# A two-layer mixer block on one core: VectorE's convolution sums in PSUM, the convolution's chunks projected ahead of the pool's, and 15 of 31 taps on GpSimd

## The chip, the cores and the metric

One NeuronCore of a Trainium2 chip runs the whole program in one launch. The metric is the device time of that launch in microseconds (us), the median of several runs. Engines are named as in the profile: PE is TensorE, DVE is VectorE, ACT is ScalarE, POOL is GpSimd, SP starts the transfers.

## What is computed

A sequence of 256 tokens with 2048 features passes two layers. Each is a mixer and a gated feed-forward block with residual sums and RMS norms. The change touches only the mixer of the first layer:

```python
def conv_pool_mixer(x, norm_g, w_in, conv_w, conv_b, ln_g, ln_b, w_pool, pool_scale, w_out):
    h = rms_norm(x, norm_g)
    u = h @ w_in
    a_val = u[..., :D_CONV]
    a_gate = u[..., D_CONV:2 * D_CONV]
    b_in = u[..., 2 * D_CONV:]
    a = a_val * jax.nn.sigmoid(a_gate)
    a = causal_depthwise_conv(a, conv_w) + conv_b
    a = jax.nn.silu(layer_norm(a, ln_g, ln_b))
    p = multiscale_pool(b_in, w_pool, pool_scale)
    return jnp.concatenate([a, p], axis=-1) @ w_out
```

D_CONV is 1024 and the causal convolution has 31 taps. The pool makes windowed means (2, 4, 8, 16 tokens) minus the value, in four groups of 256 features, and each group has a 256x256 product of its own.

## The kernel before

Features lie along the 128 partitions and the 256 tokens along the free dimension, so an activation of 2048 features is 16 chunks of 128x256. Weights come as 128x128 blocks in fp32, in the order of their use. A piece of 8 blocks is split by ACT into a rounded half (`hi`, line 109) and by DVE into the rest (`lo = w - hi`, line 110). In the first mixer a block costs PE three products of 256 columns: hi*hi (line 155), hi*lo (156) and lo*hi (157). So PE can't finish a block before DVE has made the `lo` of its piece. Six buffers each hold `hi` and `lo` pieces: `hi` of piece i can be written when PE is done with piece i-6. Pieces 0 to 2 hold 1, 3 and 4 blocks, all later ones 8, so that piece i is PE's stretch number i-2 of 8 blocks, counted from 0. Below, a "stretch of eight" is such a stretch.

The first mixer has 656 blocks, 82 stretches of eight. Stretches 0 to 7 are the four first chunks (value and gate of convolution chunks 0 and 1). Then `M0_ORDER` (line 34) says in which order the other chunks of the first product come: a convolution chunk is a value and a gate accumulator (two stretches each), a pool group is two accumulators. Stretches 48 and 49 are the pool's own products from `cat` (line 448), 50 to 65 the half of the output projection that reads the pool (`project(xs, ...)`, line 497), 66 to 81 the half that reads the convolution (line 500). The feed-forward block begins behind them with PE's first product of line 152.

The other engines work beside that:

- `gated` (line 403): DVE scales value and gate out of PSUM (line 310), ACT takes the sigmoid, DVE multiplies both into `a_in` (line 407).
- The convolution of a pair of chunks is cut in two. For its first taps ACT multiplies (`prod`, line 364, four buffers) and POOL adds to `conv` in SBUF (line 366). For the others DVE multiplies and adds in one instruction into `side` (line 377; the first tap is line 375). Line 381 adds `side` to `conv`.
- `pooled` (line 418): DVE scales out of PSUM into `xp` (line 425), makes the windowed sums (`sw`, lines 430 to 434), ACT rounds to `cat` (line 436) and DVE makes the rest (line 437). PE's stretches 48 and 49 read `cat`; their results go to `xs` by ACT (line 188) and DVE (line 189).
- The layer norm of the convolution (lines 457 to 485) runs beside stretches 50 to 65 and ends with Silu on ACT (line 482), `cat` (line 484) and its rest on DVE (line 485). Stretch 66 reads it.

`CONV` (line 76) says how many taps of which chunks go to POOL; `PACE` (line 77) how many blocks of products are issued between two steps of the side work. A scheduler orders each engine's instructions from that; each engine then runs its list in order. [...]

Of the kernel before, what the change touches and what calls it, by code (L numbers as in the profile page):

```python
# [11 lines left out]
F32 = mybir.dt.float32  # L12
# [5 lines left out]
P = 128  # L18
T = 256
# [11 lines left out]

# the order of the first product's output after its first four chunks: chunks of the convolution,
# and groups of the pool
M0_ORDER = (
    ("conv", 2), ("conv", 3), ("pool", 3), ("conv", 4), ("conv", 5), ("pool", 2), ("conv", 6),
    ("pool", 1), ("pool", 0), ("conv", 7),
)
POOL_ORDER = [i for kind, i in M0_ORDER if kind == "pool"]
POOL_CHUNKS = [2 * g + j for g in POOL_ORDER for j in range(2)]

# columns of the per-feature vectors, one column per chunk of 128 features
VECS = {}
# [9 lines left out]

# blocks of 128x128 weights in the order of their use
N_BLOCKS = 24 * NC + 16 + NC * NC + 2 * (2 * NF * NC + NC * NF) + 48 * NC + NC * NC
# [10 lines left out]
UNIT_AT = [sum(UNITS[:u]) for u in range(len(UNITS))]  # L65
# units are split into halves in pieces: (unit, first block, blocks)
PIECE = 8
PIECES = [(u, o, min(PIECE, n - o)) for u, n in enumerate(UNITS) for o in range(0, n, PIECE)]
# pieces that are split, and units that are loaded, before they are needed
LOOK = 4  # L70
AHEAD = 1
# products that the tensor engine turns over before the first operands are there
WARM = 9
# taps of each pair of chunks of the long convolution that GpSimd adds up (VectorE takes the rest),
# and the pace of the work beside the matrix products in blocks a step
CONV = {1: (0, 2, 20), 3: (2, 2, 20), 5: (4, 2, 19), 6: (6, 1, 18), 7: (7, 1, 18)}
PACE = {"pool2": 4.6, "dve2": 6.5, "pool1": 2.5, "dve1": 2.2, "ln": 4.0, "wait": 1.0, "now": 0.0}


@with_exitstack  # L80
def block_kernel(ctx: ExitStack, tc: tile.TileContext, xT: bass.AP, vec: bass.AP, wall: bass.AP, out: bass.AP):
# [5 lines left out]
    tmp = ctx.enter_context(tc.tile_pool(name="tmp", bufs=2))  # L87
    ps = ctx.enter_context(tc.tile_pool(name="ps", bufs=7, space=PSUM))
    ps_st = ctx.enter_context(tc.tile_pool(name="ps_st", bufs=1, space=PSUM))

# [1 line left out]
    loaded, ready = {}, {}  # L92
    cursor = [0, 0]  # next block, piece of the next block

# [33 lines left out]

# [1 line left out]
    queues = {name: deque() for name in ("pool", "dve", "ln", "wait")}  # L130
# [28 lines left out]
    def matmul_chunks(xs, ks, n=1, wide=False, behind=None):  # L159
        """n chunks of 128 output features: hi*hi + hi*lo + lo*hi. When wide, columns 0:T hold  # L160
        hi*hi and T:2T the cross terms."""
        accs = [ps.tile([P, 2 * T], F32, name="acc") for _ in range(n)]
        for i, k in enumerate(ks):
            first, last = i == 0, i == len(ks) - 1
            for acc in accs:
                hi, lo = next_block()
                product(acc, hi, lo, xs[:, k, :], first, last, wide)
                tick()
            if behind is not None:
                behind(k)  # L170
        return accs

    phase = [None]  # the pool of the part of the kernel that is being built

# [7 lines left out]
    def split(dst, src, scale=None):  # L182
        """dst[:, :T], dst[:, T:] = fp32r halves of src (times a scale per feature)."""
        if scale is None:
            nc.scalar.copy(dst[:, :T], src)
            nc.vector.tensor_tensor(out=dst[:, T:], in0=src, in1=dst[:, :T], op=ALU.subtract)
        else:
            nc.scalar.activation(dst[:, :T], src, AF.Copy, scale=scale)  # L188
            nc.vector.scalar_tensor_tensor(out=dst[:, T:], in0=src, scalar=scale, in1=dst[:, :T], op0=ALU.mult, op1=ALU.subtract)

# [1 line left out]
    v = const.tile([P, NVEC], F32, name="v")  # L192
# [8 lines left out]
    nc.gpsimd.memset(ones, 1.0)  # L201
    # the tensor engine's clock rises after some microseconds of work
    idle = ps_st.tile([P, P], F32, name="idle", tag="st")
# [13 lines left out]
    def rsqrt_of(*totals, scale, halves=False):  # L217
        """(scale * sum over features and over totals + EPS) ** -0.5 per token, in every partition,
        if asked for in two halves. Tokens lie along the partitions in between."""
        st = ps_st.tile([P, 2], F32, name="st", tag="st")  # L220
# [19 lines left out]
    def over_features(x):  # L240
        """Sum over the partitions, in every partition."""
        st = ps_st.tile([P, T], F32, name="st", tag="st")
        nc.tensor.matmul(st, ones, x, start=True, stop=True)
        return st

    class Norm:
        """RMS norm: h * gain goes into xs chunk by chunk; the factor per token follows."""

# [28 lines left out]
        def square2(self, c):  # L277
            """A pair of chunks."""
            into = tmp.tile([P, 2, T], F32, name="sum2" if c == 0 else "sq2", tag="sum2" if c == 0 else "gate", bufs=1 if c == 0 else 2)
            nc.scalar.activation(into, h[:, c : c + 2, :], AF.Square)  # L280
            if c:
                nc.gpsimd.tensor_tensor(out=self.pairs, in0=self.pairs, in1=into, op=ALU.add)
            else:
                self.pairs = into
                self.sums = [into[:, 0, :], into[:, 1, :]]
# [7 lines left out]
    def project(src, ks, norm=None, wide=False, narrow_end=False):  # L293
        """h += src @ weights, and the next norm behind it."""
        for n in range(NC):
            if narrow_end and n == NC - 1:
                wide = False
            (acc,) = matmul_chunks(src, ks, wide=wide)
            if wide:
                t = phase[0].tile([P, T], F32, name="cross", bufs=3)  # L300
                nc.scalar.copy(t, acc[:, T:])
                nc.vector.tensor_tensor(out=h[:, n, :], in0=h[:, n, :], in1=t, op=ALU.add)
            nc.vector.tensor_tensor(out=h[:, n, :], in0=acc[:, :T], in1=h[:, n, :], op=ALU.add)
            if norm is not None:
                norm.add(n)
# [9 lines left out]

# [1 line left out]
    norm = Norm("mix_norm_e")  # L317
# [27 lines left out]
    every = range(NC)  # L345
    with tc.tile_pool(name="m0", bufs=1) as m0:
        pad = CW - 1
# [8 lines left out]
        def tap(c, n, k):  # L356
            """GpSimd's taps of n chunks."""
            dst = conv[:, c : c + n, :] if k == 0 else m0.tile([P, 2, T], F32, name="prod", bufs=4)[:, :n, :]
# [9 lines left out]
        def side_tap(c, n, k, first):  # L368
            """VectorE's taps, in a sum of their own."""
            if k == first:  # L370
                sides[c] = m0.tile([P, 2, T], F32, name="side", bufs=2)
            for j in range(n):
                src, wt, dst = a_in[:, c + j, k : k + T], col("conv_w_e", (c + j) * CW + k), sides[c][:, j, :]
                if k == first:
                    nc.vector.tensor_scalar(out=dst, in0=src, scalar1=wt, scalar2=None, op0=ALU.mult)  # L375
                else:
                    nc.vector.scalar_tensor_tensor(out=dst, in0=src, scalar=wt, in1=dst, op0=ALU.mult, op1=ALU.add)  # L377
# [11 lines left out]
        def convolve(c, n, taps):  # L389
            """The causal convolution of n chunks."""  # L390
            left = [2]
# [5 lines left out]

            later("pool", f"pool{n}", *(partial(tap, c, n, k) for k in range(taps)))
            later("dve", f"dve{n}", *(partial(side_tap, c, n, k, taps) for k in range(taps, CW)))
            for name in ("pool", "dve"):  # L400
# [17 lines left out]
        def pooled(g):  # L418
            """Windowed means minus the value, for a group of the pool."""
            w = WINDOWS[g]  # L420
# [29 lines left out]

        # layer norm over the features of the convolution, beside the pool's output projection
        state = {}
# [66 lines left out]

# [1 line left out]
    after = Norm("mix_norm_o")  # L521
    swiglu(norm, after)

# [1 line left out]
    norm = Norm("ffn_norm1")  # L525
# [25 lines left out]

# [1 line left out]
    last = Norm("final_norm", final=True)  # L553
# [17 lines left out]
def _blocks(w):  # L571
    """[K, N] -> [N/128, K/128, 128, 128]: output chunk, input chunk, input, output."""
    k, n = w.shape
# [3 lines left out]
def _cols(a):  # L577
    """[N] -> [128, N/128]"""
    return a.reshape(-1, P).T
# [69 lines left out]
```

## Time and profile before

| | before |
|---|---|
| median of 3 runs | 2149.49 us (2149.3 to 2149.75) |
| profiled execution, first to last instruction | 2148.9 us |
| PE busy in it | 2095.9 us, 98% |
| DVE, ACT, POOL busy | 1456.4, 1068.2, 202.2 us |

The page gives the span of the profiled execution and no time of its own for what lies around the span; the median of the runs is 0.6 us above it. Of the span, the first mixer takes the first 306.5 us; there PE is not always busy, and from there to the end it is.

### The profile page before, as it was taken

To read this page: it belongs to the slowest core of one execution; us is meant where nothing else is said; L and a number is where in the kernel's file an instruction comes from. 1 tells how busy PE (TensorE), PEld (TensorE's weight loads), DVE (VectorE), ACT (ScalarE), POOL (GpSimd) and SP (SyncE) were. 2 spreads that over 40 slices of the span, in tenths; PEclk is the share of its full clock that TensorE was granted. 3 is DMA by queue.
4 is the path that set the end of the run, shared out by engine and by line. 5 is a ranking of instruction groups with operands and counts; after the bars stand their busy time and mean duration, and the time that the engine had idled before them with its cause. 6 is when DMAs were issued, how large, how long until landed. Compare 5 with 4: busy or idle time off the path is not lost.

```text
span 2148.9 us, 31546 instructions
## 1 busy us (share of the span) xinstructions
PE 2095.9 (98%) x12564; PEld 1869.5 (87%) x12564; DVE 1456.4 (68%) x1952; ACT 1068.2 (50%) x1595; POOL 202.2 (9%) x210
## 2 busy tenths in 40 slices
PE   8787999999999999999999999999999999999997
PEld 8787998888888888888888888888888888888887
DVE  7999886666555666666677777766666556666554
ACT  7655665444444444445444444554444444444553
POOL 3766420000000000001000000100000000000011
PEclk9889999999999999999999999999999999999999
DMA  7234455555555555555455555555555555555551
GB/s 280 83 134 157 160 200 190 187 186 196 187 186 195 183 190 196 185 188 194 179 196 184 189 197 184 188 184 189 196 187 187 195 180 193 196 184 189 196 180 75
DMA packets 56851, 393.43 MB, mean 183 GB/s; under 512 B 6400, under 2 KB 7424, under 8 KB 9984
## 3 DMA queue, kind: packets, MB, share of 16 engines
q1 hardware_dynamic: 56704, 391.42, 51.1%
q8 instruction: 98, 1.61, 0.3%
q14 instruction: 49, 0.40, 0.1%
HBM read 389.30 MB, written 2.10 MB: 182 GB/s over the span
## 4 chain that ended last, share of the span: by engine, by line
PE 89%; DVE 8%; issue 1%; ACT 1%; DMA 0%; SPq 0%; DVEq 0%
PE acc L152 56%; PE acc L153 29%; DVE side L377 3%; DVE lo L110 2%; PE acc L157 1%; PE acc L156 1%; PE acc L155 1%; DVE sw L430 0%; ACT xs L188 0%; ACT hi L109 0%; DMA h<-in_xT 0%; DVE a_in L407 0%; DVE h L559 0%; DVE side L375 0%; DVE conv L381 0%
## 5 line engine op out<-in xcount | busy, mean ns | idle before, releaser
L110 DVE TENSOR_TENSOR lo<-w,hi 128x1024 fp32r<-128x1024 f32 (+1 forms) x740 | 921.9, 1247 | 632.5 <-ACT hi L109 628.7
L109 ACT CAST hi<-w 128x1024 fp32r<-128x1024 f32 (+1 forms) x740 | 775.7, 1050 | 949.1 <-PE acc L152 622.4
L152 PE MATMUL acc<-xs,hi 128*128 128x512 f32 x3584 | 1243.3, 391 | 0.0
L153 PE MATMUL acc<-xs,lo 128*128 128x256 f32 x3584 | 1003.9, 280 | 0.0
L152 PEld LDWEIGHTS acc<-xs,hi 128*128 128x128 f32 x3584 | 670.3, 187 | 146.9
L153 PEld LDWEIGHTS acc<-xs,lo 128*128 128x128 f32 x3584 | 677.3, 189 | 0.1
L152 PE MATMUL acc<-y,hi 128*128 128x512 f32 x1386 | 485.2, 393 | 0.0
L153 PE MATMUL acc<-y,lo 128*128 128x256 f32 x1386 | 386.1, 279 | 0.0
L152 PEld LDWEIGHTS acc<-y,hi 128*128 128x128 f32 x1386 | 259.4, 187 | 62.1
L153 PEld LDWEIGHTS acc<-y,lo 128*128 128x128 f32 x1386 | 259.7, 187 | 0.4
L273 POOL TENSOR_TENSOR sumsq<-sumsq,sq 128x256 f32<-128x256 f32 x56 | 57.5, 1026 | 1587.8 <-ACT sq L271 1587.8
L157 PE MATMUL acc<-xs,lo 128*128 128x256 f32 x512 | 150.3, 302 | 31.4 <-DVE lo L110 31.2
L155 PE MATMUL acc<-xs,hi 128*128 128x256 f32 x512 | 151.3, 299 | 3.3 <-ACT hi L109 3.3
L156 PE MATMUL acc<-xs,hi 128*128 128x256 f32 x512 | 150.6, 297 | 0.0
L157 PEld LDWEIGHTS acc<-xs,lo 128*128 128x128 f32 x512 | 103.7, 206 | 34.5 <-DVE lo L110 34.3
L366 POOL TENSOR_TENSOR conv<-conv,prod 128x512 f32<-128x512 f32 (+1 forms) x90 | 124.0, 1379 | 62.8 <-ACT prod L364 56.9
L155 PEld LDWEIGHTS acc<-xs,hi 128*128 128x128 f32 x512 | 105.8, 207 | 3.8 <-ACT hi L109 3.7
L156 PEld LDWEIGHTS acc<-xs,hi 128*128 128x128 f32 x512 | 105.7, 207 | 0.1
L152 PE MATMUL acc<-z,hi 128*128 128x512 f32 x256 | 89.6, 393 | 0.0
L177 ACT COPY cross<-acc 128x256 f32<-128x256 f32 x224 | 81.7, 365 | 0.0
L377 DVE SCALAR_TENSOR_TENSOR side<-a_in,v,side 128x256 f32<-128x256 f32 x86 | 77.3, 919 | 0.4
L153 PE MATMUL acc<-z,lo 128*128 128x256 f32 x256 | 71.3, 279 | 0.0
(116 smaller groups left out, 1172.9 us busy)
## 6 DMA issues: line engine op xcount, KB each, us to landing
w<-in_wall SPq DMA_DIRECT2D x365, 1024.0 KB, 4.8
w<-in_wall SPq DMA_DIRECT2D x7, 512.0 KB, 7.1
h<-in_xT SPq DMA_DIRECT2D x7, 256.0 KB, 7.2
out<-h SPq DMA_DIRECT2D x3, 512.0 KB, 2.7
v<-in_vec SPq DMA_DIRECT2D x1, 260.0 KB, 6.6
h<-in_xT SPq DMA_DIRECT2D x2, 128.0 KB, 2.6
w<-in_wall SPq DMA_DIRECT2D x1, 256.0 KB, 3.9
out<-h SPq DMA_DIRECT2D x2, 128.0 KB, 1.9
```

Of the source, the lines that this page charges most:

```text
L109: nc.scalar.copy(hi[:, : n * P], w)
L110: nc.vector.tensor_tensor(out=lo[:, : n * P], in0=w, in1=hi[:, : n * P], op=ALU.subtract)
L152: nc.tensor.matmul(acc, hi, x, start=first, stop=False, skip_group_check=True)
L153: nc.tensor.matmul(acc[:, T:], lo, x[:, :T], start=False, stop=last, skip_group_check=True)
L155: nc.tensor.matmul(acc[:, :T], hi, x[:, :T], start=first, stop=False)
L156: nc.tensor.matmul(acc[:, :T], hi, x[:, T:], start=False, stop=False)
L157: nc.tensor.matmul(acc[:, :T], lo, x[:, :T], start=False, stop=last)
L177: nc.scalar.copy(t, acc[:, T:])
L273: nc.gpsimd.tensor_tensor(out=self.sums[0], in0=self.sums[0], in1=sq, op=ALU.add)
L366: nc.gpsimd.tensor_tensor(out=conv[:, c : c + n, :], in0=conv[:, c : c + n, :], in1=dst, op=ALU.add)
L377: nc.vector.scalar_tensor_tensor(out=dst, in0=src, scalar=wt, in1=dst, op0=ALU.mult, op1=ALU.add)
```

## The change

`side` moves from SBUF to PSUM: a pool of two banks, open during the first mixer alone. For that the accumulators get five banks instead of seven, in the whole kernel. `M0_ORDER` puts all convolution chunks ahead of all pool groups (the weights lie in memory in that order, so that transfers are the same). `CONV` makes four pairs of chunks of 15 POOL taps and 16 DVE taps each, where it had three pairs (20, 20 and 19 taps on POOL) and two single chunks (18 each). So POOL adds 56 times 512 columns (before: 56 times 512 and 34 times 256), and DVE makes 128 side taps of 256 columns (before: 94). `PACE` follows.

```diff
 M0_ORDER = (
-    ("conv", 2), ("conv", 3), ("pool", 3), ("conv", 4), ("conv", 5), ("pool", 2), ("conv", 6),
-    ("pool", 1), ("pool", 0), ("conv", 7),
+    ("conv", 2), ("conv", 3), ("conv", 4), ("conv", 5), ("conv", 6), ("conv", 7), ("pool", 3),
+    ("pool", 2), ("pool", 1), ("pool", 0),
 )
...
-CONV = {1: (0, 2, 20), 3: (2, 2, 20), 5: (4, 2, 19), 6: (6, 1, 18), 7: (7, 1, 18)}
-PACE = {"pool2": 4.6, "dve2": 6.5, "pool1": 2.5, "dve1": 2.2, "ln": 4.0, "wait": 1.0, "now": 0.0}
+CONV = {1: (0, 2, 15), 3: (2, 2, 15), 5: (4, 2, 15), 7: (6, 2, 15)}
+PACE = {"pool": 6.8, "dve": 6.4, "ln": 3.0, "wait": 1.0, "now": 0.0}
...
-    ps = ctx.enter_context(tc.tile_pool(name="ps", bufs=7, space=PSUM))
+    ps = ctx.enter_context(tc.tile_pool(name="ps", bufs=5, space=PSUM))
...
-    with tc.tile_pool(name="m0", bufs=1) as m0:
+    with tc.tile_pool(name="m0", bufs=1) as m0, tc.tile_pool(name="ps_side", bufs=2, space=PSUM) as ps_side:
...
-                sides[c] = m0.tile([P, 2, T], F32, name="side", bufs=2)
+                sides[c] = ps_side.tile([P, 2, T], F32, name="side")
```

The instruction lists of all engines are the same before the first side taps and from the feed-forward block on. Three places in between matter below. The first is ACT in the convolution: how many `prod` (two make one POOL add) stand between two `hi` casts. Before, at the third pair:

```order
L362 ACTIVATE conv<-a_in,v 128x256
L364 ACTIVATE prod<-a_in,v 128x256 x6
L109 CAST hi<-w 128x1024 x2
L364 ACTIVATE prod<-a_in,v 128x256 x4
L109 CAST hi<-w 128x1024
L364 ACTIVATE prod<-a_in,v 128x256 x4
```

Now, at the second pair:

```order
L362 ACTIVATE conv<-a_in,v 128x256
L364 ACTIVATE prod<-a_in,v 128x256 x2
L109 CAST hi<-w 128x1024
L364 ACTIVATE prod<-a_in,v 128x256 x4
L109 CAST hi<-w 128x1024
L364 ACTIVATE prod<-a_in,v 128x256 x4
```

The rate there is four `prod`, two adds, a piece in both. Now all 112 `prod` stand between the casts of pieces 17 and 47, about two adds a piece for 30 pieces; before, they ran on among the later pieces.

The second place is DVE at the end of the pool, just ahead of PE's stretches 48 and 49. Before, the last chunk there was a convolution chunk (`val`, `gate`), and the last group's `cat` was done ahead of its gate:

```order
L310 TENSOR_TENSOR val<-acc,rstd 128x256
L377 SCALAR_TENSOR_TENSOR side<-a_in,v,side 128x256
L434 SCALAR_TENSOR_TENSOR pm<-sw,xp 128x512
L110 TENSOR_TENSOR lo<-w,hi 128x1024
L381 TENSOR_TENSOR conv<-conv,side 128x256
L437 TENSOR_TENSOR cat<-pm,cat 128x2x256
L387 TENSOR_TENSOR total<-total,conv 128x256
L110 TENSOR_TENSOR lo<-w,hi 128x1024
L310 TENSOR_TENSOR gate<-acc,rstd 128x256
```

Now the last group's sums and the `cat` of the two last groups come behind its last accumulator, with side taps and a `lo` between them:

```order
L430 TENSOR_TENSOR sw<-xp 128x2x256
L377 SCALAR_TENSOR_TENSOR side<-a_in,v,side 128x256 x2
L434 SCALAR_TENSOR_TENSOR pm<-sw,xp 128x512
L189 SCALAR_TENSOR_TENSOR xs<-acc,v,xs 128x256
L432 TENSOR_TENSOR sw<-sw,corr 128x2
L377 SCALAR_TENSOR_TENSOR side<-a_in,v,side 128x256 x2
L110 TENSOR_TENSOR lo<-w,hi 128x1024
L189 SCALAR_TENSOR_TENSOR xs<-acc,v,xs 128x256
L434 SCALAR_TENSOR_TENSOR pm<-sw,xp 128x512
L437 TENSOR_TENSOR cat<-pm,cat 128x2x256
L377 SCALAR_TENSOR_TENSOR side<-a_in,v,side 128x256 x2
L437 TENSOR_TENSOR cat<-pm,cat 128x2x256
```

The third place is ACT at the end of the layer norm, ahead of PE's stretch 66. Before, the last `hi` in front of Silu was that of piece 71, and two more stood among the casts to `cat`:

```order
L109 CAST hi<-w 128x1024 x3
L482 ACT_TABLE_LOAD
L482 ACTIVATE conv<-conv,v 128x256 x6
L484 CAST cat<-conv 128x2x256
L482 ACTIVATE conv<-conv,v 128x256 x2
L109 CAST hi<-w 128x1024
L484 CAST cat<-conv 128x2x256 x2
```

Now it is that of piece 73, and none stands among the casts:

```order
L109 CAST hi<-w 128x1024 x3
L482 ACT_TABLE_LOAD
L482 ACTIVATE conv<-conv,v 128x256 x6
L484 CAST cat<-conv 128x2x256
L482 ACTIVATE conv<-conv,v 128x256 x2
L484 CAST cat<-conv 128x2x256 x3
```

So Silu now stands behind two more pieces, and the last of them takes the buffer of piece 67, which is PE's stretch 65.

## Rows read from the trace of the kernel before

**Rows 1.** The page: busy time, share of the span and instructions of each engine.

```profile
PE 2095.9 (98%) x12564; PEld 1869.5 (87%) x12564; DVE 1456.4 (68%) x1952; ACT 1068.2 (50%) x1595; POOL 202.2 (9%) x210
```

**Rows 2.** Windows: length, busy PE, PEld, DVE, ACT, POOL (instructions), granted clock, DMA.

```profile
47.66:73.58 25.92, 25.92 (x219) 25.92 (x218) 24.38 (x24) 17.09 (x35) 20.80 (x14) 1.00 0.35 111
73.58:211.80 138.22, 102.99 (x723) 99.98 (x722) 138.01 (x152) 81.60 (x153) 85.81 (x62) 0.87 0.35 125
211.80:306.50 94.70, 93.95 (x778) 93.22 (x778) 85.04 (x121) 63.22 (x102) 35.73 (x34) 0.99 0.52 185
306.50:406.50 100.00, 100.00 (x581) 88.22 (x580) 64.80 (x97) 51.34 (x75) 0.17 (x1) 1.00 0.52 184
```

**Rows 3.** Waits, 46 to 212 us: who waited for whom, total, times, longest.

```profile
PE acc L157 <- DVE lo L110: 29.3, 10, 6.2
PE acc L155 <- DVE gate L310: 4.0, 1, 4.0
```

**Rows 4.** DVE by line and shape, 46 to 212 us: busy and mean ns.

```profile
L377 DVE SCALAR_TENSOR_TENSOR side<-a_in,v,side 128x256 f32<-128x256 f32 x74 | 68.8, 955 | 0.2
L110 DVE TENSOR_TENSOR lo<-w,hi 128x1024 fp32r<-128x1024 f32 x40 | 60.8, 1521 | 0.0
L425 DVE TENSOR_TENSOR xp<-acc,rstd 128x256 f32<-128x256 f32 x8 | 3.3, 412 | 0.0
L189 DVE SCALAR_TENSOR_TENSOR xs<-acc,v,xs 128x256 fp32r<-128x256 f32 x3 | 1.3, 469 | 0.0
L387 DVE TENSOR_TENSOR total<-total,conv 128x256 f32<-128x256 f32 x1 | 0.4, 410 | 0.0
```

**Rows 5.** POOL by line and shape, 46 to 212 us.

```profile
L366 POOL TENSOR_TENSOR conv<-conv,prod 128x512 f32<-128x512 f32 x56 | 87.0, 1555 | 45.1 <-ACT prod L364 41.6
L366 POOL TENSOR_TENSOR conv<-conv,prod 128x256 f32<-128x256 f32 x17 | 19.4, 1143 | 5.5 <-ACT prod L364 4.3
```

**Rows 6.** DVE's timeline: start, us to the last end, what, how many merged.

```profile
74.88 1.21 DVE L110 TENSOR_TENSOR lo<-w,hi 128x1024 fp32r<-128x1024 f32 x1
76.02 0.41 DVE L310 TENSOR_TENSOR gate<-acc,rstd 128x256 f32<-128x256 f32 x1
76.35 1.26 DVE L377 SCALAR_TENSOR_TENSOR side<-a_in,v,side 128x256 f32<-128x256 f32 x3
77.53 1.21 DVE L110 TENSOR_TENSOR lo<-w,hi 128x1024 fp32r<-128x1024 f32 x1
...
87.66 5.77 DVE L377 SCALAR_TENSOR_TENSOR side<-a_in,v,side 128x256 f32<-128x256 f32 x4
```

**Rows 7.** PE's timeline at the starts of stretches 11 and 50 and of the feed-forward block.

```profile
47.66 0.28 PE L155 MATMUL acc<-xs,hi 128*128 128x256 f32 x1
...
211.79 0.41 PE L155 MATMUL acc<-xs,hi 128*128 128x256 f32 x1
212.01 0.41 PE L156 MATMUL acc<-xs,hi 128*128 128x256 f32 x1
...
306.48 0.40 PE L152 MATMUL acc<-xs,hi 128*128 128x512 f32 x1
```

**Rows 8.** DVE's timeline: `lo` of piece 17, up to which its list is hardly changed.

```profile
45.99 1.23 DVE L110 TENSOR_TENSOR lo<-w,hi 128x1024 fp32r<-128x1024 f32 x1
```

**Rows 9.** Timelines of DVE and ACT at the end of the layer norm.

```profile
254.69 2.50 DVE L480 TENSOR_TENSOR conv<-conv,lr 128x512 f32<-128x512 f32 x4
261.30 0.69 DVE L485 TENSOR_TENSOR cat<-conv,cat 128x512 fp32r<-128x512 f32 x1 [2.30 <-ACT cat L484]
...
255.33 1.05 ACT L109 CAST hi<-w 128x1024 fp32r<-128x1024 f32 x1 [2.26 <-PE acc L156]
257.69 3.07 ACT L482 ACTIVATE conv<-conv,v 128x256 f32<-128x256 f32 x6
260.66 0.60 ACT L484 CAST cat<-conv 128x512 fp32r<-128x512 f32 x1
265.10 0.62 ACT L484 CAST cat<-conv 128x512 fp32r<-128x512 f32 x1
```

More of the change, by code (lines that the diff above doesn't have):

```diff
@@ L396, in end @@
                     later("ln", "now", partial(convolved, c, n))
-            later("pool", f"pool{n}", *(partial(tap, c, n, k) for k in range(taps)))
-            later("dve", f"dve{n}", *(partial(side_tap, c, n, k, taps) for k in range(taps, CW)))
+            later("pool", "pool", *(partial(tap, c, n, k) for k in range(taps)))
+            later("dve", "dve", *(partial(side_tap, c, n, k, taps) for k in range(taps, CW)))
             for name in ("pool", "dve"):
```

## The prediction

> **What bounds the kernel now.** First the page: PE is busy 98% of the span [rows 1], so only the little that PE does not do can be won. The windows say where that lies. From 47.66 to 73.58 us PE runs nine stretches of eight (216 products) in 25.92 us, 2.88 us each, at the full granted clock [rows 2]. From 73.58 to 211.80 us it runs 30 stretches, which at that pace take 86.4 us, in 138.22 us: 51.8 us are lost. There DVE is busy 138.01 of the 138.22 us and the granted clock is 0.87 on the mean. From 211.80 to 306.50 us the last 32 stretches take 94.70 us, some 3 us over their pace, and behind 306.50 us PE is never idle. So the most that any change of the first mixer's middle can bring is some 52 us.
>
> Next the waits of that stretch: PE stands before its lo products, for DVE's `lo`, 29.3 us in ten waits, and 4.0 us once for an accumulator that DVE had not read [rows 3]. DVE is late. Why, the groups say: a side tap of 256 columns takes 955 ns on the mean [rows 4], but on the timeline three of them begin 0.39 us apart at 76.35 us, and four at 87.66 us 1.42 us apart ((5.77-1.5)/3) [rows 6]. At 87.66 us POOL is adding, at 76.35 us it is not. A POOL add and a DVE instruction with two operands in SBUF take turns, and a turn of POOL costs DVE 1.42-0.39 = 1.03 us for 512 columns. `lo` suffers likewise: 1521 ns on the mean [rows 4] against 1.21 at 74.88 us [rows 6]. `xp`, which reads one operand from PSUM, takes 412 ns beside the same adds [rows 4]. The excess of side taps and `lo` alone is 68.8-74x0.47 = 34 and 60.8-40x1.21 = 12 us, 46 us over 73 adds [rows 5], 0.63 us an add; with the smaller groups of that view (first taps, `a_in`, sums of 512 columns), counted in the same way, 61 us and 0.84.
>
> **The change, step by step.** The prices of DVE are spacings on the undisturbed timeline [rows 6]: `lo` 1.14 us, 256 columns of two tensors 0.33, a side tap 0.39 to 0.40, and 0.60 for 512 columns (four in 2.50 us at 254.69 us [rows 9]).
>
> 1. *Side taps in PSUM.* A tap then has one operand in SBUF, as `xp` has, so I take it out of the turns. The trace has no DVE write to PSUM. The nearest row is line 189, which reads an accumulator, multiplies and subtracts: 469 ns [rows 4], what an undisturbed side tap takes. So I take 0.396 us a tap. The cheap end is 0.33 (a plain sum of 256 columns); the dear end is 0.60, as if the read and the write of 256 columns in one bank followed each other.
>
> A tensor in PSUM costs DVE no more than one in SBUF by the rows: 412 ns for `xp`, 410 for `total` [rows 4]. [...]
>
> 2. *DVE's list without turns.* Up to `lo` of piece 17, which ends at 47.2 us [rows 8], nothing moves. From there to the `cat` of the last pool group (the last row of the second place shown) DVE has 39 `lo` (44.3 us), 97 side taps (38.4), 32 short instructions (7 first taps, 11 gates and values, 6 `a_in`, 8 `xp`: 10.7), 4 `xs` (1.6) and 21 of 512 columns (12.7), with 0.4 for the rest 108 us, so that it could be there at 155.3 us. PE at its pace has stretch 48, the first that reads `cat`, at 47.66+37x2.88 = 154.2 us [rows 2, 7].
>
> 3. *What is left of the turns.* POOL's 56 adds are all of 512 columns now. By ACT's list they come at two a piece, over 28 to 30 pieces, in which DVE itself needs 2.59 us a piece (83 us for pieces 18 to 49). Of that 1.14 for `lo` and some 0.25 for `a_in`, the sums and the pool still need their turn, so the turns want 2x1.03+1.39 = 3.45 us a piece: more than DVE's own 2.59 and than PE's 2.88. Over 28 pieces that delays DVE by 28x0.86 = 24 us at least, if every other microsecond of POOL lies beside side taps. The low end is 12 us, if part of an add's 1.03 us lies beside the end of a DVE instruction, the high end 56x1.03 = 58, if none is hidden. I take 25, near the low end, because between two `lo` there are now 1.3 us of instructions that need no turn. It is not lost at once: `lo` of piece 17 is done 12 us ahead of its stretch (15, at 59.2 us), and that lead is spent first.
>
> 4. *The end of the pool.* The lead ends at `cat`. With 25 us of turns DVE has the last `cat` at 180.3 us; PE needs 1.2 us more for it, having drawn half a stretch of the projection ahead, and stands where its pace has it at 161.5 us (stretch 50.5): 20 us late. Were DVE in time, PE would still be 5 us late, because behind the last accumulator (154.2 us) DVE has 11.1 us of its list to go, side taps and `lo` between the sums of the pool. So this stall is the larger of 5 us and (turns - 5). In the later stretches DVE regains its lead: POOL has no more adds there until the norm. For products at the lower clock behind the stall (0.22 us each at 211.79 us against 0.12 [rows 7]) the tail of before has a price already; I add 1 us for a longer stop.
>
> 5. *The layer norm.* Before, the last cast ahead of Silu began at 255.33 us [rows 9] and took the buffer of stretch 63, two stretches before PE needs `cat`. Now ACT has one cast ahead of it that needs the buffer of PE's stretch 65, the last before `cat`. So behind stretch 65 come a cast, the table load and six Silu and the first `cat`: from 255.33 to 261.26 us, 5.9 us [rows 9]. With DVE's part (0.6) and the three other pairs, spread over the first stretch, PE loses some 6.5 us. Of the 3 us that the tail of before is over its pace I put 0.5 here: 6 us more.
>
> 6. *Nothing for the rest.* Banks: five instead of seven let PE run four accumulators ahead of DVE, 23 us in the first product. I cost that at nothing, since DVE is late by less; if that cover fails, a wait is like the 4.0 us of before [rows 3]. From the feed-forward block on the lists are the same and PE is busy all the time [rows 2]. Transfers are the same. ACT has 120 instead of 154 convolution products, and was busy 81.60 of 138.22 us [rows 2].
>
> **The sum.** PE reaches stretch 50 at 160.0 us by its pace; with 20 for turns and the pool's end and 1 for the clock 181.0; the tail as before takes 94.7 us [rows 2], with 6 for the norm 281.7 us. Before, the feed-forward block began at 306.5 us [rows 7]. The gain is 24.8 us on the span of 2148.9 us; the median of the runs lies 0.6 us above that span, so 2149.5-24.8 = **2125 us**.
>
> **The rivals.**
> - *The adds hide well* (turns cost 12 us or less; the stall at the pool's end falls to 5 to 7 us): 160+6+94.7+6 = 267 us, 2110 us. For it: the turns' price was taken where both engines wanted one at any moment. Against: two adds a piece are more than the pauses between `lo` hold.
> - *PSUM in place is dear.* At 0.60 us a tap, 97 taps cost 20 us more, all on DVE ahead of the stall: 2145 us. For it: no row shows DVE reading and writing one bank. Against: line 189 and `xp`, as cheap as SBUF.
> - *A bank short.* At the pool's end eight small accumulators and the projection's share five banks that DVE empties between side taps; up to four waits like that of 4.0 us: 2141 us.
> - *Slower: every add still stops DVE for its whole turn.* Side taps no longer meet POOL, but `lo` does, and each late `lo` makes the next add meet the next one. At 1.03 us an add turns cost 58 us and the stall is 53: 160+53+1+94.7+6 = 315 us, 8 us later than before, 2158 us. It decides from 50 us on, 0.89 us an add; before, an add cost 0.84. Against: `lo` is the only long instruction left that needs a turn, 40% of DVE's time.
>
> **Chances and range.** Forecast (2117 to 2134) 0.56; adds hide well 0.16; dear PSUM 0.10; a bank short 0.10; slower 0.08. The low end of the range is a little under the second case, 2108; the high end takes in the bank's case and stops short of dear PSUM, 2142. A measurement of this kernel can tell about 0.2%, 4 us, from no change: up to 2145 us counts as faster. All of the first, second and fourth case and half of dear PSUM are faster, 0.87; the other half, 0.05, is no change; 0.08 slower.
>
> **What would show it.** In the profile after: side taps near 0.47 us and 128 of them; `lo` still above 1.21 on the mean, at some 1.5 or 1.6 us; PE without a long wait until some 155 us, then a stop of about 20 us in several waits for `cat` or `lo`; another of some 6 us ahead of the first product of `cat` by the convolution, released by ACT's or DVE's `cat`; PE's first product of line 152 at about 282 us. The prediction is wrong if side taps take more than 0.6 us, if PE stops for `lo` all through the convolution, or if it stops for banks.

## The result and the profile after

The changed kernel takes **2132.4 us** (median of 4 runs, 2131.0 to 2133.7), the kernel before, measured with it, 2149.6 us (2149.3 to 2149.8). The ratio is 0.9921 with a 95% interval of [0.9908, 0.9933]: faster by 17 us. The forecast was 2125 us, 7 us less, with a range that holds the result.

The page answers to [rows 1]; PE is busy 9 us less with the same 12564 products, since fewer of them ran at the lower clock: the granted clock is 0.98 from 73.58 to 154.20 us, where it had been 0.87 on the mean from 73.58 to 211.80 us [rows 2].

```profile
PE 2087.0 (98%) x12564; PEld 1860.7 (87%) x12564; DVE 1428.6 (67%) x1984; ACT 1057.5 (50%) x1561; POOL 179.0 (8%) x176
```

The windows of the first mixer, with the columns of [rows 2]: up to the pool's end, the pool's end, and from there to the feed-forward block.

```profile
47.66:73.58 25.92, 25.92 (x218) 25.92 (x217) 25.54 (x38) 21.68 (x41) 24.98 (x14) 1.00 0.40 140
73.58:154.20 80.62, 74.24 (x591) 72.57 (x590) 75.66 (x105) 59.74 (x109) 74.22 (x42) 0.98 0.42 146
154.20:190.00 35.80, 21.61 (x136) 20.02 (x135) 35.44 (x69) 12.68 (x19) 0.25 (x2) 0.71 0.39 144
190.00:287.45 97.45, 91.56 (x753) 91.24 (x751) 81.18 (x118) 54.82 (x80) 18.68 (x17) 0.96 0.47 170
```

Up to 154 us PE now lacks 6.4 of 80.62 us, where it had lacked a quarter of its time; at the pool's end it lacks 14, with products at the lower clock besides (0.71 granted). POOL is busy 74.22 of 80.62 us, DVE no longer all the time.

The waits of 46 to 212 us, as in [rows 3]:

```profile
ACT prod L364 <- POOL conv L366: 21.0, 34, 1.9
PE acc L155 <- ACT cat L436: 8.5, 2, 6.7
PE acc L157 <- DVE lo L110: 6.3, 7, 2.5
DVE lo L110 <- ACT hi L109: 5.1, 7, 1.9
PE acc L156 <- DVE cat L437: 3.9, 2, 2.3
PE acc L155 <- DVE xp L425: 1.6, 1, 1.6
```

PE waits for `lo` 6.3 us where it waited 29.3 [rows 3], and 14 us in all at the pool's end, nearly all for `cat`. The first row is another engine's: ACT waits 21.0 us for POOL to free one of the four product buffers. Before, that wait was short:

```profile
ACT prod L364 <- POOL conv L366: 4.6, 9, 1.0
```

DVE's groups in the same stretch, as in [rows 4], and POOL's, as in [rows 5]:

```profile
L110 DVE TENSOR_TENSOR lo<-w,hi 128x1024 fp32r<-128x1024 f32 x48 | 71.8, 1497 | 5.5 <-ACT hi L109 5.1
L377 DVE SCALAR_TENSOR_TENSOR side<-a_in,v,side 128x256 f32<-128x256 f32 x118 | 53.7, 482 | 0.3
L407 DVE TENSOR_TENSOR a_in<-val,gate 128x256 f32<-128x256 f32 x6 | 5.6, 932 | 0.0
```

```profile
L366 POOL TENSOR_TENSOR conv<-conv,prod 128x512 f32<-128x512 f32 x56 | 100.6, 1797 | 29.9 <-ACT prod L364 25.8
```

A side tap takes 482 ns on the mean where it took 955 [rows 4]; `lo` is hardly shorter, 1497 ns. POOL's add rose from 1555 [rows 5] to 1797 ns.

DVE's timeline (start, us, what, how many merged) shows both beside POOL's adds, and the end of its list for the pool:

```profile
43.27 1.22 DVE L110 TENSOR_TENSOR lo<-w,hi 128x1024 fp32r<-128x1024 f32 x1
...
127.37 1.26 DVE L377 SCALAR_TENSOR_TENSOR side<-a_in,v,side 128x256 f32<-128x256 f32 x3
129.08 1.99 DVE L110 TENSOR_TENSOR lo<-w,hi 128x1024 fp32r<-128x1024 f32 x1 [0.44 <-ACT hi L109]
...
171.74 0.76 DVE L425 TENSOR_TENSOR xp<-acc,rstd 128x256 f32<-128x256 f32 x2
...
182.52 0.70 DVE L437 TENSOR_TENSOR cat<-pm,cat 128x512 fp32r<-128x512 f32 x1
```

The first row is `lo` of piece 17, as in [rows 8]. At 127.37 us POOL is in the middle of three adds (126.58 to 132.22 us), and three taps still begin 0.39 us apart; the `lo` behind them takes 1.99 us. Then PE's timeline, which answers to [rows 7]: the starts of stretches 11, 48, 50 and 66 and of the feed-forward block, the longest stop of the pool's end, and two products in a row behind a later stop, 0.21 us apart (the scheduler mixes in products of the projection, so that a stretch is counted by products).

```profile
44.81 0.28 PE L155 MATMUL acc<-xs,hi 128*128 128x256 f32 x1
...
161.39 0.28 PE L155 MATMUL acc<-cat,hi 128*128 128x256 f32 x1
...
170.01 0.58 PE L155 MATMUL acc<-cat,hi 128*128 128x256 f32 x1 [6.68 <-ACT cat L436]
...
182.27 0.42 PE L157 MATMUL acc<-cat,lo 128*128 128x256 f32 x1
182.48 0.41 PE L155 MATMUL acc<-cat,hi 128*128 128x256 f32 x1
...
186.75 0.41 PE L156 MATMUL acc<-xs,hi 128*128 128x256 f32 x1
...
240.33 0.58 PE L155 MATMUL acc<-cat,hi 128*128 128x256 f32 x1 [5.89 <-ACT cat L484]
...
287.45 0.40 PE L152 MATMUL acc<-xs,hi 128*128 128x512 f32 x1
```

From stretch 11 to the feed-forward block it took 242.6 us, before 258.8 (306.48-47.66 [rows 7]). Against its pace of 2.88 us PE lost 10.0 us up to stretch 48 (116.6-37x2.88), 19.6 us in stretches 48 and 49 (25.4-5.76), and 8.5 us in the last 32 (100.7-92.2).

### The profile page after: what moved, and what is told of

Read it like the earlier page. It is cut to its first block, busy times and chain, and to the rows that moved or that the text cites. A ratio compares the mean times of both kernels' runs of the same rounds, so it can differ in the third digit from the quotient of the medians.

```text
span 2130.1 us, 31502 instructions
## 1 busy us (share of the span) xinstructions
PE 2087.0 (98%) x12564; PEld 1860.7 (87%) x12564; DVE 1428.6 (67%) x1984; ACT 1057.5 (50%) x1561; POOL 179.0 (8%) x176
## 4 chain that ended last, share of the span: by engine, by line
PE 92%; POOL 3%; DVE 2%; ACT 1%; issue 1%; DMA 0%; SPq 0%; POOLq 0%; DVEq 0%
PE acc L152 56%; PE acc L153 29%; POOL conv L366 3%; PE acc L157 2%; PE acc L156 2%; PE acc L155 2%; DVE lo L110 1%; ACT prod L364 1%; DMA w<-in_wall 0%; DVE side L377 0%; DVE sw L430 0%; ACT hi L109 0%; DVE h L559 0%; PE st L223 0%; DVE xs L189 0%
## 5 line engine op out<-in xcount | busy, mean ns | idle before, releaser
L152 PEld LDWEIGHTS acc<-xs,hi 128*128 128x128 f32 x3584 | 670.3, 187 | 147.1
L155 PE MATMUL acc<-xs,hi 128*128 128x256 f32 x512 | 145.6, 287 | 1.7 <-ACT hi L109 1.7
L156 PE MATMUL acc<-xs,hi 128*128 128x256 f32 x512 | 145.1, 286 | 0.0
L366 POOL TENSOR_TENSOR conv<-conv,prod 128x512 f32<-128x512 f32 x56 | 100.6, 1797 | 29.9 <-ACT prod L364 25.8
L155 PEld LDWEIGHTS acc<-xs,hi 128*128 128x128 f32 x512 | 99.7, 195 | 2.2 <-ACT hi L109 2.1
L156 PEld LDWEIGHTS acc<-xs,hi 128*128 128x128 f32 x512 | 99.7, 195 | 0.1
L364 ACT ACTIVATE prod<-a_in,v 128x256 f32<-128x256 f32 x112 | 50.8, 501 | 21.4 <-POOL conv L366 21.0
```

Source lines behind the costliest of these rows:

```text
L152: nc.tensor.matmul(acc, hi, x, start=first, stop=False, skip_group_check=True)
L155: nc.tensor.matmul(acc[:, :T], hi, x[:, :T], start=first, stop=False)
L156: nc.tensor.matmul(acc[:, :T], hi, x[:, T:], start=False, stop=False)
L364: nc.scalar.activation(dst[:, j, :], src, AF.Copy, scale=wt)
L366: nc.gpsimd.tensor_tensor(out=conv[:, c : c + n, :], in0=conv[:, c : c + n, :], in1=dst, op=ALU.add)
```

## The experiments

Each kernel was made from the one before or from the changed one by the edit shown; since a scheduler orders the lists, an edit shifts them a little, and each run is read from its own trace. Times are medians; "lost" is the time that PE took beyond its pace of 2.88 us a stretch, counted as above: from stretch 11 to 48, in stretches 48 and 49, and from stretch 50 to the feed-forward block. The starting point, stretch 11, lay between 44.7 and 48.0 us in the profiled executions without the kernel's doing (45.1 us in the run with five banks, whose lists there are those of before, and which was not faster), so that the losses are compared, not the absolute moments.

| kernel | us | lost to stretch 48 | in 48 and 49 | behind | sum |
|---|---|---|---|---|---|
| before | 2149.6 | 44.2 | 7.6 | 2.5 | 54 |
| changed | 2132.4 | 10.0 | 19.6 | 8.5 | 38 |
| before, five banks | 2150.0 | 44.2 | 10.0 | 1.3 | 56 |
| before, side taps in PSUM | 2126.7 | 14.1 | 15.6 | 1.6 | 31 |
| changed, side taps in SBUF | 2167.5 | 43.0 | 20.8 | 8.2 | 72 |
| PSUM, new order, old taps | 2135.4 | 12.6 | 26.4 | 0.4 | 39 |
| PSUM, old order, new taps | 2132.1 | 5.1 | 9.7 | 22.4 | 37 |
| changed, 12 POOL taps | 2135.3 | 0.9 | 19.0 | 20.5 | 40 |
| changed, eight product buffers | 2128.7 | 9.7 | 16.4 | 6.8 | 33 |
| changed, adds of 32 columns | 2112.8 | 0 | 9.7 | 7.7 | 17 |

**The parts of the change.** First PSUM alone, in the kernel before (the accumulators get five banks here too):

```diff
-    ps = ctx.enter_context(tc.tile_pool(name="ps", bufs=7, space=PSUM))
+    ps = ctx.enter_context(tc.tile_pool(name="ps", bufs=5, space=PSUM))
...
-                sides[c] = m0.tile([P, 2, T], F32, name="side", bufs=2)
+                sides[c] = ps_side.tile([P, 2, T], F32, name="side")
```

> The kernel before with one part of the change alone: VectorE's sums in two PSUM banks (so five for accumulators); order, taps and pace as before. Theory (side taps leave the turns with GpSimd's adds): a side tap takes 0.48 us on the mean instead of 0.92, 94 of them give VectorE some 38 us; the turns with lo stay, and GpSimd's 90 adds become the next limit. Gain 10 to 25 us, about 2130. Rival (the order and the number of taps bring the gain, PSUM by itself little, since lo then meets the adds in the side taps' place): within 5 us of 2149.6.

Measured: 2126.7 us (2125.9 to 2128.3), ratio 0.9898 [0.9883, 0.9913]. This one edit gives at least as much as the whole change, some 22 us against 17, though the intervals of the two ratios overlap from 0.9908 to 0.9913. Its side taps take 480 ns. The three rows of its waits that matter, 46 to 212 us:

```profile
ACT prod L364 <- POOL conv L366: 30.8, 40, 1.8
PE acc L157 <- DVE lo L110: 9.4, 8, 2.9
PE acc L155 <- DVE val L310: 7.4, 1, 7.4
```

The last is a bank: PE needs the one that holds the last convolution chunk's value, and DVE comes late to it; one more such wait, for a gate, takes 2.9 us. Next the reverse, the changed kernel with `side` back in SBUF (two buffers) and five banks as they were:

> The changed kernel with VectorE's sums back in SBUF (accumulators stay at five banks). Theory: 128 side taps meet 56 adds again, an add costs VectorE 0.84 to 1.03 us instead of some 0.45, 20 to 33 us more: 2150 to 2165, no faster than before. Rival (the gain is from order and taps): 2130 to 2140.

Measured: 2167.5 us (2166.4 to 2167.9), ratio 1.0087 [1.0070, 1.0104]. Without PSUM the rest of the change makes the kernel slower than before, a little more so than the theory had it. Its DVE groups of 46 to 212 us say why:

```profile
L377 DVE SCALAR_TENSOR_TENSOR side<-a_in,v,side 128x256 f32<-128x256 f32 x110 | 85.0, 812 | 0.0
L110 DVE TENSOR_TENSOR lo<-w,hi 128x1024 fp32r<-128x1024 f32 x39 | 57.3, 1468 | 0.0
```

More taps on DVE, 812 ns each, and PE waits 27.1 us for `lo`, as long as before. Then the banks alone, five instead of seven in the kernel before:

> The kernel before with five accumulator banks instead of seven and nothing else. Theory: no cost, 2147 to 2152. Rival (banks short at the pool's end or in the feed-forward blocks): 3 us or more slower, with more waits of TensorE for an accumulator than the 4 us and 2 us of before.

Measured: 2150.0 us (10 runs, 2148.9 to 2150.6), ratio 1.0004 [0.9995, 1.0013]: the two banks cost nothing there. A wait for `val` of 3.2 us appears beside that for `gate` (3.3), and the losses add up to the same within 1.2 us.

Now the order and the split of the taps, each alone on top of PSUM. The order:

```diff
-    ("conv", 2), ("conv", 3), ("pool", 3), ("conv", 4), ("conv", 5), ("pool", 2), ("conv", 6),
-    ("pool", 1), ("pool", 0), ("conv", 7),
+    ("conv", 2), ("conv", 3), ("conv", 4), ("conv", 5), ("conv", 6), ("conv", 7), ("pool", 3),
+    ("pool", 2), ("pool", 1), ("pool", 0),
```

> The kernel before with the side taps in PSUM and the new order of the chunks (all convolution chunks ahead of the pool), but with the old split of taps (94 on DVE, 90 adds on POOL) and the old pace. Theory (POOL sets the pace of the convolution, through ACT's four product buffers and the casts to hi behind them): the adds of 56x512 and 34x256 columns now follow each other without a pause, at 1.87 and some 1.4 us an add, 150 us from 46 to 196 us, beyond the pool's cat; PE reaches stretch 48 no earlier than in the changed kernel (161.4 us), rather at 165 to 172, stops again behind the last accumulator, and has almost no stop at the layer norm, since Silu stands behind the cast of piece 67; 2125 to 2140 us. Rival (the new order is what gains, the new split of taps is what costs): stretch 48 at 155 to 160 us and 2115 to 2124 us, faster than the 2126.7 of the run with PSUM alone.

Measured: 2135.4 us (2133.6 to 2137.4), ratio 0.9933 [0.9918, 0.9948]. The theory held, but for 1 us: stretch 48 at 164.0 us, a long stop behind it, no stop at the norm. Its two main waits of 46 to 212 us:

```profile
ACT prod L364 <- POOL conv L366: 35.0, 51, 1.7
PE acc L155 <- ACT cat L436: 19.4, 2, 14.9
```

Then the changed kernel with the old order, which leaves the new split of taps alone on top of PSUM:

> The changed kernel with the old order of the chunks (pool groups between the convolution chunks): the new split of taps and PSUM, without the new order. Theory: the 56 adds are spread over the whole first product, POOL pauses, and stretch 48 comes at 152 to 158 us instead of 161.4; but the last pair of chunks is complete only with the last chunk of the first product, so 14 adds and 32 taps begin behind it, some 26 us of POOL, and the layer norm comes later: PE stops ahead of stretch 66 longer than the 6.5 us of the changed kernel, 8 to 20 us; 2125 to 2140 us. Rival (the order only moves a stall from one place to another): the same as the changed kernel within 3 us, 2129 to 2135.

Measured: 2132.1 us (2130.9 to 2132.6), ratio 0.9916 [0.9899, 0.9932]. Stretch 48 came at 158.1 us, at the edge of the theory's range, and stretch 66 late by 20.6 us, a little over it; the total fits both theories, since what is saved in one place is lost in the other. In 212 to 300 us PE waits for the statistics of the norm:

```profile
PE st L223 <- DVE total L473: 7.3, 1, 7.3
PE st L243 <- DVE total L458: 3.9, 1, 3.9
PE acc L155 <- ACT cat L484: 3.9, 1, 3.9
```

So with PSUM the four combinations are: old order and taps 2126.7, new order 2135.4, new taps 2132.1, both 2132.4 us. The order costs 8.7 us with the old taps and nothing with the new ones. That the new taps cost 5 us with the old order is likely, but not shown: the intervals overlap ([0.9899, 0.9932] and [0.9883, 0.9913]).

**Less for POOL.** The changed kernel with `CONV` at 12 POOL taps instead of 15:

> The changed kernel with 12 GpSimd taps a pair instead of 15: 44 adds instead of 56, 152 side taps instead of 128. Theory (GpSimd runs without a pause at 1.87 us an add, ScalarE waits 21 us for product buffers, and lo is late through the casts behind it): TensorE reaches the pool's products 3 to 7 us earlier than at 161.4 us, ScalarE's waits for GpSimd nearly go. VectorE has 24 taps more, 9.5 us, and 12 turns of some 0.45 us less, 5 us: its end of the pool moves by 0 to +4 us, so that the time is the same or up to 4 us slower, 2131 to 2137. Rival (GpSimd alone is the limit): 7 to 15 us faster, 2118 to 2125.

Measured: 2135.3 us (2134.0 to 2137.5), ratio 0.9938 [0.9923, 0.9953]. PE reached stretch 48 at 152.1 us, 9 us earlier, and lost that again: the convolution's last side taps, in the trace up to 222 us, ran into the norm (20.5 us behind stretch 50). So the time is the theory's, but not the way to it, which had the loss at the end of the pool.

**POOL through ACT.** The changed kernel with deeper buffers between ACT and POOL:

```diff
-m0.tile([P, 2, T], F32, name="prod", bufs=4)
+m0.tile([P, 2, T], F32, name="prod", bufs=8)
```

> The changed kernel with eight product buffers between ACT and POOL instead of four. Theory (the 10 us lost ahead of the pool's end come from ACT, which waits for POOL with casts to hi behind it): ACT's waits for POOL fall from 21.0 to under 10 us, stretch 48 comes 3 to 8 us earlier than 161.4 us; a part of it is taken back at the pool's end, and 2127 to 2131 us are left. Rival (DVE's list with its turns is late by itself, whatever ACT does): stretch 48 within 1.5 us of 161.4, the time within 2 us of 2132.

Measured: 2128.7 us (2126.2 to 2130.1), ratio 0.9901 [0.9886, 0.9915]. In 46 to 212 us:

```profile
ACT prod L364 <- POOL conv L366: 15.6, 14, 1.9
DVE lo L110 <- ACT hi L109: 2.7, 2, 1.9
```

The time is where the theory put it, and from stretch 11 to the feed-forward block 237.4 us against 242.6. But stretch 48 came at 161.1 us, where the rival had it, and ACT's waits fell only to 15.6: PE got the time back behind the start of stretch 48, since DVE's last `cat` ended at 179.73 us instead of 183.22. So the coupling costs some 4 us by the medians, though not at the place that I had named; the intervals of the two ratios overlap. The same edit on the kernel with PSUM alone:

> The kernel before with the side taps in PSUM, the old order, the old taps and pace, and eight product buffers instead of four. Theory (as in the changed kernel, the deeper buffers free the casts to hi from POOL, and some 3 to 4 us of it reach the end): ACT's waits for POOL fall from 30.8 to under 20 us, stretch 50 at 183 to 188 us instead of 189.8, 2120 to 2125 us. Rival (here DVE is busy all the time anyway from 74 us on, so that ACT's waits cost nothing): 2126 to 2128 us.

Measured: 2129.1 us (2127.4 to 2130.4), ratio 0.9906 [0.9890, 0.9923], not told apart from 2126.7: no gain, and neither forecast. DVE's wait for `hi` was only 2.9 us there, and stays at 2.4; ACT still waits 24.8 us for POOL, where the theory wanted under 20. The trace shows two changes that cancel: up to stretch 50 it lost 27.5 us instead of 29.7, and behind it 5.3 instead of 1.6, where Silu stood behind one more cast to `hi`, that of piece 72 instead of 71. So this run does not show that ACT's waits cost nothing there.

**The adds nearly taken away.** The changed kernel with POOL's adds cut to 32 of their 512 columns, so that the sums leave out the other 480:

```diff
...
-nc.gpsimd.tensor_tensor(out=conv[:, c : c + n, :], in0=conv[:, c : c + n, :], in1=dst, op=ALU.add)
+nc.gpsimd.tensor_tensor(out=conv[:, c : c + n, :16], in0=conv[:, c : c + n, :16], in1=dst[:, :, :16], op=ALU.add)
```

> The changed kernel with POOL's adds cut to 32 of their 512 columns; the other columns of the products are left out of the sum. The order of the lists shifts a little, the end of the pool and Silu's place stay as they are. Theory (the stop of PE up to stretch 50 is DVE's turns with POOL, as the sum of the prediction has it, plus some 5 us at the pool's end): without turns DVE follows PE, stretch 48 at 151 to 154 us, stretch 50 at 160 to 165 us instead of 186.7; the tail of 100.7 us stays, so the first product of line 152 comes at 261 to 266 us, 2104 to 2110 us. Rival (DVE's own list is too long, and POOL is a small part of its lateness): stretch 50 later than 172 us and 2117 us or more.

Measured: 2112.8 us (2111.8 to 2114.2), ratio 0.9829 [0.9814, 0.9843], between the two forecasts. DVE's and POOL's groups of 46 to 212 us:

```profile
L110 DVE TENSOR_TENSOR lo<-w,hi 128x1024 fp32r<-128x1024 f32 x54 | 66.0, 1225 | 3.0 <-ACT hi L109 2.5
L377 DVE SCALAR_TENSOR_TENSOR side<-a_in,v,side 128x256 f32<-128x256 f32 x120 | 54.9, 482 | 0.5
...
L366 POOL TENSOR_TENSOR conv<-conv,prod 128x32 f32<-128x32 f32 x56 | 27.8, 497 | 78.1 <-ACT prod L364 76.7
```

`lo` falls to 1225 ns, its price without turns; the side taps stay at 482 ns, to which full adds had added nothing. PE runs from stretch 11 to 48 without any loss (48.0 to 154.5 us), and yet the stretches 48 and 49 lose 9.7 us:

```profile
161.77 0.80 PE L155 MATMUL acc<-cat,hi 128*128 128x256 f32 x2 [2.45 <-ACT cat L436]
165.09 0.58 PE L156 MATMUL acc<-cat,hi 128*128 128x256 f32 x1 [2.53 <-DVE cat L437]
```

So the adds, with the turns and with ACT's waits for POOL, which go as well here, cost the changed kernel 19.9 us up to stretch 50 (29.6-9.7). The list behind the last accumulator costs 9.7 us by itself, the lower clock behind its stops included (0.75 on the mean from 154 to 166 us).

**Looking for a better version**, from the kernel with PSUM alone, `PACE` rescaled each time (not shown): two taps of each chunk fewer on POOL; one fewer, with eight product buffers; and, with the taps below, the last convolution chunk ahead of the last pool group.

```diff
-CONV = {1: (0, 2, 20), 3: (2, 2, 20), 5: (4, 2, 19), 6: (6, 1, 18), 7: (7, 1, 18)}
+CONV = {1: (0, 2, 18), 3: (2, 2, 18), 5: (4, 2, 17), 6: (6, 1, 16), 7: (7, 1, 16)}
```

> The kernel before with the side taps in PSUM (2126.7 us in the run above) and two taps of each chunk fewer on POOL (18, 18, 17 of the pairs, 16 of the single chunks; DVE 10 more taps of two chunks), the pace rescaled. Theory (POOL is the limit there, DVE has room since its taps are out of the turns): seven fewer adds of 512 columns and so on, 12 us less of POOL, 8 us more of DVE; stretch 48 at 160 to 165 us instead of 168.4, 2118 to 2125 us. Rival (DVE is the limit): stretch 48 later than 168.4 and 2128 to 2136 us.

Measured: 2128.7 us (2128.0 to 2129.5), ratio 0.9902 [0.9887, 0.9917]. Up to stretch 50 it lost 25.4 us instead of 29.7, but Silu then stood behind two more casts, and 9.5 us were lost behind stretch 50 instead of 1.6. Less POOL did help ahead of the pool's end, as the theory had it; the time is the rival's.

```diff
+CONV = {1: (0, 2, 19), 3: (2, 2, 19), 5: (4, 2, 18), 6: (6, 1, 17), 7: (7, 1, 17)}
```

> The same with eight product buffers and one tap of each chunk fewer on POOL (19, 19, 18 of the pairs, 17 of the single chunks), the pace rescaled. Theory (between the run with the old taps, which lost time at the pool's end, and that with two taps fewer, which lost it at the layer norm): stretch 50 at 180 to 186 us, a stop of 0 to 5 us ahead of stretch 66, 2118 to 2124 us. Rival (what is won ahead of the pool's end is lost at the norm, as with two taps fewer): 2125 to 2130 us.

Measured: 2129.4 us (2127.5 to 2131.1), ratio 0.9906 [0.9891, 0.9920]: the rival, with 9.3 us lost behind.

```diff
-    ("conv", 2), ("conv", 3), ("pool", 3), ("conv", 4), ("conv", 5), ("pool", 2), ("conv", 6),
-    ("pool", 1), ("pool", 0), ("conv", 7),
+    ("conv", 2), ("conv", 3), ("pool", 3), ("conv", 4), ("conv", 5), ("pool", 2), ("conv", 6), ("pool", 1), ("conv", 7),
+    ("pool", 0),
...
+CONV = {1: (0, 2, 18), 3: (2, 2, 18), 5: (4, 2, 18), 6: (6, 1, 16), 7: (7, 1, 16)}
```

> The kernel before with the side taps in PSUM and one exchange in its order: the last convolution chunk comes ahead of the last pool group; POOL takes 18 taps of the pairs and 16 of the single chunks (with two taps fewer and the old order: 2128.7 us, stretch 50 at 183.2, and about 7 us lost at the norm, where Silu stood behind the cast of piece 73). Here Silu stands behind that of piece 70. Theory (the stop at the norm is set by the place of Silu among the casts; the stop at the pool's end by DVE's lateness, which stays about the same): stretch 50 at 182 to 188 us, at most 1 us lost ahead of stretch 66, 2118 to 2124 us. Rival (what is taken from the norm comes back at the pool's end, since the last chunk's taps and adds now lie ahead of the last cat, as with the new order and the old taps): stretch 50 at 190 us or later, 2125 to 2133 us.

Measured: 2128.4 us (2126.8 to 2128.8), ratio 0.9902 [0.9886, 0.9919]: the rival again. The stop at the norm was gone (stretch 66 began 2.9 us behind stretch 65), as it should be if Silu's place among the casts sets it; but stretches 48 and 49 lost 19.2 us. In 46 to 212 us:

```profile
PE acc L155 <- ACT cat L436: 4.3, 1, 4.3
PE acc L155 <- DVE xp L425: 4.1, 1, 4.1
```

None of these beats PSUM alone. All the kernels with side taps in PSUM and full adds lose 31 to 40 us, only in different places.

## Why the prediction was right, and what was mis-sized

**The mechanism was right.** A side tap with its sum in PSUM is out of the turns: 482 ns beside POOL's adds and beside adds of 32 columns alike, 0.39 us from start to start. The run with PSUM alone and the run without it show that this step makes the whole gain: 22 us in the old kernel (2148.9-2126.7, both from one series), 35 in the new (2167.5-2132.4). The five banks for accumulators cost the old kernel nothing (ratio 1.0004). The order and the taps, which the prediction did not price apart from it, probably give some 6 us of it back (2132.4-2126.7; the intervals of the two ratios overlap a little). `lo`, with both its operands in SBUF, stayed in the turns: with full adds and with adds of 32 columns it takes 1497 and 1225 ns on the mean, the tap 482 and 482. Why the place of the sum decides it, no run shows.

*Step 1* held: 0.396 us a tap was taken. The rival of a dear PSUM is out: the tap's 482 ns stand against 469 for line 189 [rows 4].

*Steps 2 to 4* were 8.6 us short in their sum: 29.6 us lost up to stretch 50, where 21 were forecast. Two terms make that up. The first is **the 25 us for turns**. DVE's list from the end of `lo` of piece 17 to that of the last `cat` took 183.22-44.49 = 138.7 us, 30.7 more than the 108 without turns. Turns are 23 of them, worked out from the groups as an estimate, against the prices that the run with adds of 32 columns or a plain instruction shows: 14 in `lo` (48x(1.50-1.21)), 3 in `a_in` (6x(0.93-0.42)), 6 in the sums and the rest. The term itself was right. But 4.9 us more, up to that `cat`, are DVE's waits for `hi` (5.1 in all), and here **step 6** failed: "ACT has 120 instead of 154 convolution products" was no reason to cost ACT at nothing. With the pauses of before gone POOL is saturated, 1.87 us from add to add, ACT waits at the four product buffers, and the casts to `hi` stand behind in its list. Eight buffers took the waits for `hi` to 2.7 us and gave 3.7 us back by the medians. Of the 2.8 us that are left of the 30.7, a wait of DVE for one gate accumulator at 47.90 us takes 1.4; the rest is open.

The second is **the end of the pool**: step 4 let PE reach stretch 50 0.7 us behind the last `cat`; in the trace it is 3.5 us (186.75-183.22), and with adds of 32 columns 3.5 as well. Behind a stop the products come at 0.21 us instead of 0.12 (the granted clock is 0.50 from 182 to 186 us), and those of the last `cat` are still to be done; the 1 us put for the clock was too little. So without any turns that place costs 9.7 us, where "PE would still be 5 us late" stood.

*Where it was lost* was half wrong too. "The lead ends at `cat`" put all 21 us there. In fact `lo` ran out of its lead first: PE lost 10.0 us ahead of stretch 48, in seven waits for `lo` from 117.98 to 148.52 us (6.3 us) and in slower products behind them (granted clock 0.62 from 150 to 154 us). From stretch 11 up to the first of them it did not stop, so that the prediction's sign of being wrong, stops for `lo` all through the convolution, did not come. That does not change the sum.

*Step 5* held: the tail was 100.7 us, 94.7 [rows 2] and 6; the stop 5.89 us, released by ACT's `cat`, forecast 5.9. Over all runs what PE loses just ahead of stretch 66 goes with Silu's place: nothing where it stood behind the cast of piece 67 or 70, 0.3 to 0.8 us behind 71, 3.7 behind 72, 5.1 to 7.4 behind 73, and 19 to 21 in the two runs (12 POOL taps; new taps in the old order) where the last taps came late too.

*The sum*: stretch 50 at 181.0 us was forecast, it came at 186.75: 8.6 us later for the two terms, 2.85 earlier because stretch 11 began at 44.81 instead of 47.66. The feed-forward block followed at 287.45, forecast 281.7. The rest took 1842.6 us, before 1842.4. The last 1.7 us lie between span and median: it stood 0.6 us above the profiled span before, now 2.3.

*The rivals.* Adds hidden well: no, the turns were 23 us, not 12. A bank short: the five banks cost the old kernel nothing, and in the changed kernel one wait of 1.6 us is such a wait. With PSUM alone in the old order such waits take 10.3 us (7.4 and 2.9), so that this rival is small here, but not everywhere. That each add stops DVE for its whole turn: not on the mean, 23 us on 56 adds are 0.41 us an add, under the 0.89 from which that case would have decided.

## What to carry to other kernels

Where VectorE and GpSimd take turns, look for the accumulator that could lie in PSUM: here that took the side taps out of the turns (482 ns where they had taken 955, against 469 for line 189 [rows 4]), and the accumulators' two banks were not missed (2150.0 us with five, ratio 1.0004). Try such an edit alone before the work is shared out anew around it; here the new order and split brought nothing, and probably cost some us (2132.4 us with them, 2126.7 without). And when an engine loses its pauses, follow who fills its buffers: what stands behind the filler in its list can be late next (here ACT's casts to `hi`, for which DVE waited 5.1 us).

## What was not expected of the hardware

The first tap, a multiplication of one tensor by a scalar, has one operand in SBUF, and yet it took turns with POOL as long as its result lay in SBUF too. Of the eight before, five met no add and took 336 to 346 ns; three met one and took 1378 to 1389. With the result in PSUM all eight take 473 to 484 ns, the six that meet an add like the others (shortest, median and longest ns, first before, then after):

```profile
L375 DVE TENSOR_SCALAR side<-a_in,v x8: 336/344/1389, 45.1 to 211.3; 128x256 f32<-128x256 f32 x8
...
L375 DVE TENSOR_SCALAR side<-a_in,v x8: 473/478/484, 42.5 to 150.8; 128x256 f32<-128x256 f32 x8
```

So undisturbed it became 134 ns dearer between the medians, and beside adds 0.9 us cheaper. What makes it dearer undisturbed, no run shows.

The multiply-and-add, with its two tensors, lost next to nothing: 482 against 469 for line 189 [rows 4]. POOL pays for the turns as well: an add that starts before the DVE instruction that it meets takes 1.30 us (at 57.11 us, ahead of the `lo` of 57.43), one that starts during its turn 2.16 (at 58.48, with that `lo` up to 59.49). The mean is 1797 ns, and 1555 before [rows 5], when POOL had pauses. So freeing DVE's taps from POOL did not free POOL from the rest of DVE's list.
